# Where the output products stand among the seven products of a channel mixer's group

## The chip, the cores and the metric

The kernel runs on one core of a Trainium2 chip. The core has a matrix engine (TensorE, PE in the profile, with its weight loads as PEld), a vector engine (VectorE, DVE), a scalar engine (ScalarE, ACT), GpSimd (POOL) and SyncE (SP), which here only issues transfers. Each engine works through its own list of instructions in order; one waits for another through semaphores. The metric is the time of one execution on the device in microseconds (us), lower is better.

## The reference

A decoder trunk of two layers on a sequence of 256 positions and a width of 1024, in float32. Each layer has a token mixer beside a cross-attention into 256 memory tokens, then a dense channel mixer, and after each a layer norm:

```python
sub = jnp.concatenate([mix, mem_out], axis=-1) @ w_mix_out[i]
x = layer_norm(ALPHA * x + sub, ln_mix_g[i], ln_mix_b[i])
x = layer_norm(ALPHA * x + swiglu(x, w_ffn_in[i], w_ffn_out[i]), ln_ffn_g[i], ln_ffn_b[i])

def swiglu(x, w_in, w_out):
    g, u = jnp.split(x @ w_in, 2, axis=-1)
    return (jax.nn.silu(g) * u) @ w_out
```

The hidden width of the channel mixer is 2816, eleven chunks of 256. The change concerns `swiglu` alone, in both layers.

## The kernel before

**Splitting.** Every float32 operand of a matmul is split into a high and a low float32r part: ScalarE copies the source into the high part (`split`, L229) and VectorE subtracts it from the source for the low part (L230). A product of two split operands takes three matmuls (`PASSES`). Weights come as units of 1 MB (`raw_...`, 128 x 2048), and each unit is split in two halves of 128 x 1024 (`spl_...`). `Stream` hands them out: the order of all halves is fixed in advance by `weight_halves`, which reads the list of steps, ten split halves can stand at a time (`HALF_BUFS`), and the load of a unit is issued as soon as its raw buffer is free (`load_ahead`). So VectorE and ScalarE work ahead of TensorE by up to ten halves.

**The channel mixer** (`Ffn`, tiles end in f in the first layer and in g in the second). `ffn_steps` writes the list of steps, which `run` carries out. Chunks 0, 1 and 10 are plain ("r" steps, `chunk_in`: tiles pf, pg). Chunks 2 to 9 go in four groups of two ("s" steps, `product`): seven products M1 to M7 stand for the eight of a 2 x 2 block product. Each product is two halves, 12 matmuls of 128 x 512. Three PSUM tiles take them: M2 goes to Y, M5 and M3 to Z, and M1, M6, M7 and M4 all to X. X is added to in place, and is read between the products:

```python
if m == "M1":
    self.m1 = kept("m1", self.X)          # ScalarE copy, L592
elif m == "M2":
    nc.vector.tensor_add(self.m1, self.m1, self.Y)      # L600
elif m == "M6":
    u2 = kept("u2", self.X)               # ScalarE copy, L592
    nc.vector.tensor_add(u2, u2, self.Z)  # L604
elif m == "M7":
    nc.vector.tensor_add(self.m5, self.m5, self.X)      # L607
elif m == "M4":
    nc.scalar.activation(sg, self.X, AF.Silu)           # L610
```

So M7 cannot add to X before ScalarE has copied it into u2, and M4 not before VectorE has added it to m5. The weights of M5, M6 and M4 are sums of quarters of the weight matrix, made in place on VectorE over 128 x 2048 (L184); M7's second quarter is added to its raw tile by a GpSimd transfer (L187). Quarters 11 and 21 have one raw buffer each; the others and the output weights share a ring of four.

**Output products** ("out" steps, `chunk_out`). The hidden values of a chunk are transposed ("tp") and multiplied by the output weights, in two steps for each chunk (c.0 and c.1), each one half and 12 matmuls, into four PSUM tiles (fof, fog) that stay open over the whole mixer. They read nothing of the group that they stand in: only hidden values of chunks before it.

**Order.** TensorE's instructions run in the order of the list. Those of the other engines and the transfers are put in order when the kernel is built, by a scheduler that follows the list and its own estimates; no line of the kernel sets it.

Of the kernel before, what the change touches and what calls it, by code (L numbers as in the profile page):

```python
# [50 lines left out]
def ffn_steps(l):  # L51

    steps, due, prev = [], [], []
    for kind, c in PLAN:
        new = [("out", p, k, (0, 1)) for p in prev for k in range(2)]
        if kind == "S":

            ins = [("s", c, m) for m in PRODUCTS]
            steps += [ins[0], ("tp",), *due, ins[1], *new[:-1][:1], *ins[2:4], *new[:-1][1:], *ins[4:]]
            due = new[-1:]  # L60
        else:
            ins = [("r", c, i, (0, 1)) for i in range(4)]
            if l == 1 and c == 0:

                steps += [*(("r", 0, i, (0,)) for i in range(4)), *(("r", 1, i, (0,)) for i in range(2)), ("x",)]
            elif l == 1 and c == 1:
                steps += [*(("r", 1, i, (0,)) for i in range(2, 4)), *(("r", 0, i, (1,)) for i in range(4)),
                          *(("r", 1, i, (1,)) for i in range(2)), ("tp",), *(("r", 1, i, (1,)) for i in range(2, 4)), *new]
            elif c == NFF - 1:
                steps += [ins[0], ("tp",), *due, *ins[1:], *(("out", NFF - 3, k, (0,)) for k in range(2)), ("tp",)]  # L70
            elif c:
                steps += [ins[0], ("tp",), ins[1], *new[:1], ins[2], *new[1:], ins[3]]
            else:
                steps += ins
        prev = [c, c + 1] if kind == "S" else [c]
    return steps


def weight_halves():

    e = [(f"v{i}", x) for i in range(4) for x in range(2)]

    def both(names):
        return [(n, x) for n in names for x in range(2)]

    def ffn(l):
        h = []
        for st in ffn_steps(l):
            k = None
            if st[0] == "r":  # L90
                k = (f"r{l}_{st[1]}_{'AB'[st[2] // 2]}", st[2] % 2)
            elif st[0] == "s":
                h += [(f"s{l}_{st[1]}", st[2], x) for x in range(2)]
            elif st[0] == "out":
                k = (f"w{l}_{st[1]}", st[2])
            if k and k not in h:
                h.append(k)
        return h + [k for k in both([f"w{l}_{c}" for c in range(NFF - 3, NFF)]) if k not in h]

    e += both(("qm0", "u0", "u1", "u2", "km0", "vm0", "o0_0", "o0_1", "o0_2", "o0_3", "km1", "vm1"))  # L100
    e += ffn(0)
    e += both(("bv0", "bv1", "bv2", "bv3", "qm1", *(f"qk{i}" for i in range(6)), "o1_0", "o1_1", "o1_2", "o1_3"))
    return e + ffn(1)
# [113 lines left out]
def build(nc, tc, ins, out):  # L217
    ET = mybir.EngineType
    with (
# [302 lines left out]
        class Ffn:  # L522
# [107 lines left out]
            def run(self, mid=None):  # L630
                for st in ffn_steps(self.l):
                    self.tp_tiles()
                    if st[0] == "r":
                        self.chunk_in(*st[1:])
                        if st[1:3] == (NFF - 1, 0):
                            stream.held = {"gb", "vbig"}
                            self.gb = load_gb(self.l, "ffn")
                    elif st[0] == "s":
                        self.product(*st[1:])
                    elif st[0] == "x":  # L640
                        mid()
                    elif st[0] == "tp":
                        if self.pending:
                            self.transposes()
                    else:
                        self.chunk_out(*st[1:])
                return self.gb
# [346 lines left out]
```

## Time and profile before

| what | us |
|---|---|
| median of 3 runs (587.42 to 589.22) | 588.98 |
| the profiled execution | 589.02 |
| span of its instructions | 587.3 |
| TensorE busy | 559.6 |
| VectorE busy | 501.2 |
| ScalarE busy | 360.0 |
| mean granted clock of TensorE | 0.995 |

The span goes from the first to the last instruction; 1.7 us of the execution lie outside it. Times in a timeline are us from the start of the span. A row of a timeline merges like instructions that follow each other: its second number is the time from the first start to the last end, and what stands in brackets is the idle time of the engine before it and what ended that. The group of chunks 4 and 5 of the first layer reaches from 154.4 to 187.8 us, the four groups of the first layer from 129.6 to 255 us, and those of the second from 420.7 to 548 us.

### The profile page before, as it was taken

The numbers are of one execution on the slowest core, as the hardware profiler recorded it, in microseconds if no ns is written. First come the engines' busy times: TensorE is split into PE (matmuls) and PEld (weight loads), VectorE is DVE, ScalarE is ACT, GpSimd is POOL, SyncE is SP. The second block draws the span as 40 slices with busy tenths as digits, with TensorE's granted clock in tenths as the row PEclk, the third lists the DMA queues.
The fourth block names the chain that finished last, engine by engine and source line by source line (L and its number), as shares of the span: only waits on it lengthen the run. The fifth ranks groups of instructions, "written<-read, shape, count | busy, mean of one in ns | idle before, by whom it ended". The sixth has DMA issues, their size and how long they took to land.

```text
span 587.3 us, 8087 instructions
## 1 busy us (share of the span) xinstructions
PE 559.6 (95%) x3064; PEld 478.5 (81%) x3064; DVE 501.2 (85%) x639; ACT 360.0 (61%) x550; POOL 21.8 (4%) x32
## 2 busy tenths in 40 slices
PE   8999999999898989989999999999988989899994
PEld 7999879887786868778999998788876868687784
DVE  5797989998999989864987887499999989899726
ACT  6757958666766657642476979375567467477400
POOL 2020000000000000000100000000000000000001
PEclk9999999999999999999999999999998999999999
DMA  8996777447676694863476232335376684857102
GB/s 288 397 368 246 261 296 259 172 81 286 166 287 183 215 278 152 288 214 143 148 287 256 100 111 105 143 145 214 73 282 148 224 261 160 295 147 286 60 1 72
DMA packets 21335, 118.88 MB, mean 202 GB/s; under 512 B 2352, under 2 KB 5552, under 8 KB 8880
## 3 DMA queue, kind: packets, MB, share of 16 engines
q1 hardware_dynamic: 19856, 109.72, 51.0%
q0 software_dynamic: 1152, 8.39, 7.8%
q8 instruction: 24, 0.39, 0.3%
q10 hardware_dynamic: 288, 0.26, 0.1%
q14 instruction: 15, 0.12, 0.1%
HBM read 117.31 MB, written 1.05 MB: 202 GB/s over the span
## 4 chain that ended last, share of the span: by engine, by line
PE 79%; DVE 12%; ACT 3%; issue 3%; DMA 2%; SPq 0%; POOLq 0%; ACTq 0%; DVEq 0%
PE fof L253 10%; PE fog L253 7%; PE Xg L253 6%; PE pf L253 6%; PE Xf L253 6%; PE opc L253 4%; PE opa L253 4%; PE qk L253 3%; DVE spl_s_M L230 3%; PE Zf L253 3%; PE pg L253 3%; PE pu L253 3%; PE bv L253 3%; PE Zg L253 3%; PE pvm L253 3%
## 5 line engine op out<-in xcount | busy, mean ns | idle before, releaser
L230 DVE TENSOR_TENSOR spl_s_M<-raw_s,spl_s_M 128x1024 fp32r<-128x1024 f32 x112 | 131.8, 1219 | 8.6 <-ACT spl_s_M L229 8.6
L229 ACT CAST spl_s_M<-raw_s 128x1024 fp32r<-128x1024 f32 x112 | 112.1, 1048 | 40.9 <-DVE raw_s L184 16.2
L253 PE MATMUL fof<-spl_w,htf 128*128 128x512 f32 x264 | 63.2, 392 | 0.0
L253 PEld LDWEIGHTS fof<-spl_w,htf 128*128 128x128 f32 x264 | 49.1, 188 | 10.0
L230 DVE TENSOR_TENSOR spl_w<-raw_w,spl_w 128x1024 fp32r<-128x1024 f32 x44 | 53.3, 1218 | 4.4 <-ACT spl_w L229 4.3
L184 DVE TENSOR_TENSOR raw_s<-raw_s,raw_s 128x2048 f32<-128x2048 f32 x24 | 54.9, 2286 | 0.2
L253 PE MATMUL fog<-spl_w,htg 128*128 128x512 f32 x228 | 54.5, 392 | 0.0
L229 ACT CAST spl_w<-raw_w 128x1024 fp32r<-128x1024 f32 x44 | 46.0, 1053 | 9.5 <-PE Xf L253 3.4
L253 PEld LDWEIGHTS fog<-spl_w,htg 128*128 128x128 f32 x228 | 42.4, 188 | 8.7
L253 PE MATMUL qk<-x2T,spl_qk 128*128 128x256 f32 x288 | 36.7, 285 | 0.0
L253 PEld LDWEIGHTS qk<-x2T,spl_qk 128*128 128x128 f32 x288 | 35.2, 192 | 0.0
L253 PE MATMUL Xg<-spl_s_M,x3T 128*128 128x512 f32 x96 | 24.7, 415 | 5.1 <-DVE m5g L607 5.1
L253 PE MATMUL Xf<-spl_s_M,x1T 128*128 128x512 f32 x96 | 23.1, 395 | 5.6 <-DVE m5f L607 5.6
L253 PEld LDWEIGHTS Xg<-spl_s_M,x3T 128*128 128x128 f32 x96 | 18.9, 200 | 10.8 <-DVE m5g L607 6.8
L253 PE MATMUL Xg<-spl_s_M,SgM 128*128 128x512 f32 x96 | 23.6, 395 | 3.5 <-ACT u2g L592 3.5
L253 PEld LDWEIGHTS Xf<-spl_s_M,x1T 128*128 128x128 f32 x96 | 17.7, 188 | 10.8 <-DVE m5f L607 7.3
L253 PE MATMUL Xf<-spl_s_M,SfM 128*128 128x512 f32 x96 | 23.6, 395 | 2.7 <-ACT u2f L592 2.7
L253 PEld LDWEIGHTS Xg<-spl_s_M,SgM 128*128 128x128 f32 x96 | 17.7, 188 | 8.8 <-ACT u2g L592 5.2
L253 PEld LDWEIGHTS Xf<-spl_s_M,SfM 128*128 128x128 f32 x96 | 17.7, 188 | 7.9 <-ACT u2f L592 4.4
L253 PE MATMUL opc<-spl_o,mix 128*128 128x512 f32 x96 | 23.5, 397 | 0.0
L253 PE MATMUL Zg<-spl_s_M,SgM 128*128 128x512 f32 x96 | 23.2, 390 | 0.0
L253 PE MATMUL Zf<-spl_s_M,SfM 128*128 128x512 f32 x96 | 23.2, 390 | 0.0
(236 smaller groups left out, 1104.9 us busy)
## 6 DMA issues: line engine op xcount, KB each, us to landing
raw_s<-in_w SPq DMA_DIRECT2D x32, 1024.0 KB, 4.9
raw_w<-in_w SPq DMA_DIRECT2D x22, 1024.0 KB, 4.8
raw_o<-in_w SPq DMA_DIRECT2D x8, 1024.0 KB, 6.7
raw_s<-in_w POOLq DMA_DIRECT2D x8, 1024.0 KB, 8.3
raw_r_A<-in_w SPq DMA_DIRECT2D x6, 1024.0 KB, 4.8
raw_r_B<-in_w SPq DMA_DIRECT2D x6, 1024.0 KB, 4.7
raw_qk<-in_w SPq DMA_DIRECT2D x6, 1024.0 KB, 4.8
raw_u<-in_w SPq DMA_DIRECT2D x3, 1024.0 KB, 9.2
```

What stands on the lines that cost most here:

```text
L184: self.nc.vector.tensor_add(self.raw[parts[0]], self.raw[parts[0]], self.raw[parts[1]])
L229: nc.scalar.copy(hi, src)
L230: nc.vector.tensor_sub(lo, src, hi.bitcast(F32))
L253: nc.tensor.matmul(o, lhsT, rhs, start=start, stop=stop, skip_group_check=on)
```

## The change

Only `ffn_steps` differs. In each group the last three of the output products at hand are kept for the group's end: one stands between M6 and M7, one between M7 and M4, and one is left for the next group, behind its M1 and its transposes. The output products of chunk 0, which stood inside chunk 1 or (second layer) behind it, move into the first group. No instruction is added or taken away. The change adds five lines, so a line of the kernel before from L230 on is five higher in the changed one (L230 is L235, L600 is L605).

```diff
         if kind == "S":
             ins = [("s", c, m) for m in PRODUCTS]
-            steps += [ins[0], ("tp",), *due, ins[1], *new[:-1][:1], *ins[2:4], *new[:-1][1:], *ins[4:]]
-            due = new[-1:]
+            due += new
+            early, due = due[:-3], due[-3:]
+            steps += [ins[0], ("tp",), *early[:1], ins[1], *early[1:], *ins[2:5], due[0], ins[5], due[1], ins[6]]
+            due = due[2:]
         else:
             ...
             elif l == 1 and c == 1:
                 steps += [*(("r", 1, i, (0,)) for i in range(2, 4)), *(("r", 0, i, (1,)) for i in range(4)),
-                          *(("r", 1, i, (1,)) for i in range(2)), ("tp",), *(("r", 1, i, (1,)) for i in range(2, 4)), *new]
+                          *(("r", 1, i, (1,)) for i in range(2)), ("tp",), *(("r", 1, i, (1,)) for i in range(2, 4))]
+                due = new
             ...
             elif c:
-                steps += [ins[0], ("tp",), ins[1], *new[:1], ins[2], *new[1:], ins[3]]
+                steps += [ins[0], ("tp",), *ins[1:]]
+                due = new
```

The list for the first groups and the group of chunks 4 and 5, in both layers (outC.K is half K of the output product of chunk C):

```text
before  ... out0.0 ... out0.1 ... | M1 tp M5 out1.0 M2 M3 M6 M7 M4 | M1 tp out1.1 M5 out2.0 M2 M3 out2.1 out3.0 M6 M7 M4 | ...
after   ...                       | M1 tp out0.0 M5 M2 M3 M6 out0.1 M7 out1.0 M4 | M1 tp out1.1 M5 out2.0 M2 M3 M6 out2.1 M7 out3.0 M4 | ...
```

TensorE in the group of chunks 4 and 5 of the second layer, at the end of M6. In a name such as spl_s1_4_M6_1 stand the layer, the group, the product and the half; spl_w1_2_1 is the second half of chunk 2's output weights. Before:

```order
L253 MATMUL Xg4_4194<-spl_s1_4_M6_1_4365,SgM60_3887 128x512 x2
L253 MATMUL Xg4_4194<-spl_s1_4_M6_1_4365,SgM61_3888 128x512
L253 MATMUL Xg4_4194<-spl_s1_4_M7_0_4378,SgM70_3891 128x512 x2
L253 MATMUL Xg4_4194<-spl_s1_4_M7_0_4378,SgM71_3892 128x512
L253 MATMUL Xg4_4194<-spl_s1_4_M7_0_4378,SgM70_3891 128x512 x2
```

Now:

```order
L258 MATMUL Xg4_4196<-spl_s1_4_M6_1_4335,SgM60_3887 128x512 x2
L258 MATMUL Xg4_4196<-spl_s1_4_M6_1_4335,SgM61_3888 128x512
L258 MATMUL fog00_4011<-spl_w1_2_1_4348,htg2_4223 128x512
L258 MATMUL fog01_4012<-spl_w1_2_1_4348,htg2_4223 128x512
L258 MATMUL fog00_4011<-spl_w1_2_1_4348,htg2_4223 128x512
```

Behind M6 came M7, which adds to the same tile X; now out2.1 comes, 12 matmuls into other tiles.

VectorE in the same group, from the output halves or M3's last half to the first split of M7. Before:

```order
L230 TENSOR_TENSOR spl_w1_2_1_4325<-raw_w1_2_4179,spl_w1_2_1_4325 128x1024
L230 TENSOR_TENSOR spl_w1_3_0_4340<-raw_w1_3_4236,spl_w1_3_0_4340 128x1024
L184 TENSOR_TENSOR raw_s1_4_11_4175<-raw_s1_4_11_4175,raw_s1_4_22_4234 128x2048
L184 TENSOR_TENSOR raw_s1_4_21_4181<-raw_s1_4_21_4181,raw_s1_4_11_4175 128x2048
L230 TENSOR_TENSOR spl_s1_4_M6_0_4356<-raw_s1_4_11_4175,spl_s1_4_M6_0_4356 128x1024
L600 TENSOR_TENSOR m1g4_4215<-m1g4_4215,Yg4_4195 128x512
L230 TENSOR_TENSOR spl_s1_4_M6_1_4365<-raw_s1_4_11_4175,spl_s1_4_M6_1_4365 128x1024
L230 TENSOR_TENSOR spl_s1_4_M7_0_4378<-raw_s1_4_12_4177,spl_s1_4_M7_0_4378 128x1024
```

Now:

```order
L235 TENSOR_TENSOR spl_s1_4_M3_1_4316<-raw_s1_4_22_4183,spl_s1_4_M3_1_4316 128x1024
L189 TENSOR_TENSOR raw_s1_4_11_4175<-raw_s1_4_11_4175,raw_s1_4_22_4183 128x2048
L605 TENSOR_TENSOR m1g4_4217<-m1g4_4217,Yg4_4197 128x512
L189 TENSOR_TENSOR raw_s1_4_21_4181<-raw_s1_4_21_4181,raw_s1_4_11_4175 128x2048
L235 TENSOR_TENSOR spl_s1_4_M6_0_4326<-raw_s1_4_11_4175,spl_s1_4_M6_0_4326 128x1024
L235 TENSOR_TENSOR spl_s1_4_M6_1_4335<-raw_s1_4_11_4175,spl_s1_4_M6_1_4335 128x1024
L235 TENSOR_TENSOR spl_w1_2_1_4348<-raw_w1_2_4179,spl_w1_2_1_4348 128x1024
L235 TENSOR_TENSOR spl_s1_4_M7_0_4363<-raw_s1_4_12_4177,spl_s1_4_M7_0_4363 128x1024
```

The splits of M6 stand two halves earlier, and the addition of M2's result to m1 (which reads Y), with the sum for M4 (raw_s1_4_21) behind it, now stands ahead of M6's first split instead of behind it. The groups of chunks 6 and 8 of the second layer have the same order.

VectorE in the same group at the additions to u2 and m5. Before:

```order
L604 TENSOR_TENSOR u2g4_4374<-u2g4_4374,Zg4_4196 128x512
L184 TENSOR_TENSOR raw_s1_6_11_4410<-raw_s1_6_11_4410,raw_s1_6_12_4412 128x2048
L605 SCALAR_TENSOR_TENSOR m1g4_4215<-m1g4_4215,u2g4_4374 128x512
L607 TENSOR_TENSOR m5g4_4270<-m5g4_4270,Xg4_4194 128x512
L230 TENSOR_TENSOR spl_s1_6_M5_0_4487<-raw_s1_6_11_4410,spl_s1_6_M5_0_4487 128x1024
```

Now:

```order
L609 TENSOR_TENSOR u2g4_4344<-u2g4_4344,Zg4_4198 128x512
L235 TENSOR_TENSOR spl_w1_3_0_4382<-raw_w1_3_4236,spl_w1_3_0_4382 128x1024
L610 SCALAR_TENSOR_TENSOR m1g4_4217<-m1g4_4217,u2g4_4344 128x512
L235 TENSOR_TENSOR spl_s1_4_M4_0_4398<-raw_s1_4_21_4181,spl_s1_4_M4_0_4398 128x1024
L235 TENSOR_TENSOR spl_s1_4_M4_1_4407<-raw_s1_4_21_4181,spl_s1_4_M4_1_4407 128x1024
L612 TENSOR_TENSOR m5g4_4270<-m5g4_4270,Xg4_4196 128x512
```

Between the additions to u2 and to m5 stand three splits and one small product instead of one sum of 128 x 2048 and the small product.

## The prediction

> **What bounds the kernel now.** First the page's head, its busy times and the engines of the chain of waits:
>
> ```profile
> span 587.3 us, 8087 instructions
> PE 559.6 (95%) x3064; PEld 478.5 (81%) x3064; DVE 501.2 (85%) x639; ACT 360.0 (61%) x550; POOL 21.8 (4%) x32
> PE 79%; DVE 12%; ACT 3%; issue 3%; DMA 2%; SPq 0%; POOLq 0%; ACTq 0%; DVEq 0%
> ```
>
> TensorE carries 79% of the chain that ended last, and is idle for 587.3 - 559.6 = 27.7 us. Its own waits, longest first (us in total, times, longest):
>
> ```profile
> PE Xf L253 <- DVE m5f L607: 5.6, 4, 1.7
> PE Xg L253 <- DVE m5g L607: 5.1, 4, 2.1
> PE Xg L253 <- ACT u2g L592: 3.5, 4, 1.5
> PE Xf L253 <- ACT u2f L592: 2.7, 4, 0.7
> ```
>
> 16.9 of the 27.7 us are two waits in each of the eight groups: M7 for ScalarE's copy of X, and M4 for VectorE's addition of X to m5. What they cost in starts, the timeline of TensorE tells, here from M6 of the first layer's second group to M6 of its third, ahead of it the first group's M6, behind it the last group:
>
> ```profile
> 143.66 2.88 PE L253 MATMUL Xf<-spl_s_M,SfM 128*128 128x512 f32 x12
> ...
> 177.04 2.88 PE L253 MATMUL Xf<-spl_s_M,SfM 128*128 128x512 f32 x12
> 180.60 3.02 PE L253 MATMUL Xf<-spl_s_M,SfM 128*128 128x512 f32 x12 [0.68 <-ACT u2f L592]
> 184.91 5.74 PE L253 MATMUL Xf<-spl_s_M,x1T 128*128 128x512 f32 x24 [1.30 <-DVE m5f L607]
> 190.49 0.27 PE L620 MATMUL tpf<-ident,m1f 128*128 128x128 f32 x1
> ...
> 191.26 0.27 PE L620 MATMUL tpf<-ident,m5f 128*128 128x128 f32 x1
> ...
> 205.01 5.60 PE L253 MATMUL fof<-spl_w,htf 128*128 128x512 f32 x24
> 210.45 2.88 PE L253 MATMUL Xf<-spl_s_M,SfM 128*128 128x512 f32 x12
> ...
> 243.84 2.88 PE L253 MATMUL Xf<-spl_s_M,SfM 128*128 128x512 f32 x12
> ...
> 254.96 2.89 PE L253 MATMUL pf<-spl_r_A,x1T 128*128 128x512 f32 x12
> ```
>
> Two output products take 210.45 - 205.01 = 5.44, so a block of 12 matmuls 2.72 us. M7 starts 180.60 - 177.04 - 2.72 = 0.84 late, M4 184.91 - 180.60 - 2.72 = 1.59 late. A stretch from M6 to M6 holds eleven blocks, 29.92, and eight transposes at 0.11 (190.49 to 191.26), 0.88: 30.80 us of work. It takes 33.41. The second layer:
>
> ```profile
> 434.79 2.88 PE L253 MATMUL Xg<-spl_s_M,SgM 128*128 128x512 f32 x12
> 439.15 3.06 PE L253 MATMUL Xg<-spl_s_M,SgM 128*128 128x512 f32 x12 [1.48 <-ACT u2g L592]
> 444.31 7.33 PE L253 MATMUL Xg<-spl_s_M,x3T 128*128 128x512 f32 x24 [2.10 <-DVE m5g L607]
> ...
> 471.41 2.88 PE L253 MATMUL Xg<-spl_s_M,SgM 128*128 128x512 f32 x12
> ...
> 537.83 2.88 PE L253 MATMUL Xg<-spl_s_M,SgM 128*128 128x512 f32 x12
> 541.38 3.02 PE L253 MATMUL Xg<-spl_s_M,SgM 128*128 128x512 f32 x12 [0.68 <-ACT u2g L592]
> 545.18 3.01 PE L253 MATMUL Xg<-spl_s_M,x3T 128*128 128x512 f32 x12 [0.78 <-DVE m5g L607]
> 548.03 2.89 PE L253 MATMUL pg<-spl_r_A,x3T 128*128 128x512 f32 x12
> ```
>
> Here the first stretch takes 36.62, the two after it 33.21 each. At 444.31, 24 matmuls take 7.33 and not 5.74, and the windows by stretch show why, and VectorE beside it:
>
> ```profile
> core 0: us, PE busy (x) PEld busy (x) DVE busy (x) ACT busy (x) POOL busy (x), PEclk, DMA share, GB/s
> 440.00:450.00 10.00, 7.90 (x28) 6.02 (x27) 9.27 (x10) 5.88 (x7) 0.86 (x1) 0.83 0.81 204
> 191.53:224.95 33.42, 31.45 (x142) 25.45 (x141) 31.65 (x29) 21.24 (x26) 0.89 (x1) 1.00 0.68 220
> 485.72:518.93 33.21, 31.43 (x141) 25.44 (x141) 31.55 (x29) 21.00 (x26) 0.88 (x1) 1.00 0.69 222
> ```
>
> The granted clock falls to 0.83 there, behind two waits of 1.48 and 2.10. And VectorE is busy for 31.65 of 33.42 us of a group: it is nearly full, and needs 0.85 more than TensorE's 30.80. So the gain hangs on what VectorE lets through.
>
> **The waits that go.** An output product of 2.72 now stands ahead of M7 and another ahead of M4. Its hidden values are transposed blocks before, in the same group. What it must cover, the timeline of ScalarE and VectorE tells: the copy into u2 and the addition to m5 in the first layer's second group, the sums and splits behind them, and then, with TensorE's M3, the second layer's first and second groups:
>
> ```profile
> 179.96 0.58 ACT L592 COPY u2f<-Xf 128x512 f32<-128x512 f32 x1 [4.13 <-PE Xf L253]
> 184.18 0.68 DVE L607 TENSOR_TENSOR m5f<-m5f,Xf 128x512 f32<-128x512 f32 x1
> 194.52 4.61 DVE L184 TENSOR_TENSOR raw_s<-raw_s,raw_s 128x2048 f32<-128x2048 f32 x2
> 199.05 3.49 DVE L230 TENSOR_TENSOR spl_s_M<-raw_s,spl_s_M 128x1024 fp32r<-128x1024 f32 x3
> 428.31 4.63 DVE L230 TENSOR_TENSOR spl_s_M<-raw_s,spl_s_M 128x1024 fp32r<-128x1024 f32 x4
> 461.93 1.22 DVE L230 TENSOR_TENSOR spl_s_M<-raw_s,spl_s_M 128x1024 fp32r<-128x1024 f32 x1
> 463.25 2.88 PE L253 MATMUL Zg<-spl_s_M,SgM 128*128 128x512 f32 x12
> 463.45 0.69 DVE L600 TENSOR_TENSOR m1g<-m1g,Yg 128x512 f32<-128x512 f32 x1 [0.30 <-PE Yg L253]
> 464.06 5.76 DVE L230 TENSOR_TENSOR spl_s_M<-raw_s,spl_s_M 128x1024 fp32r<-128x1024 f32 x5
> ```
>
> M6's block is over at 177.04 + 2.72 = 179.76, ScalarE's copy of X at 180.54: 0.8 later, inside the 2.72 of the first output product. For m5, VectorE's new order puts three splits and one small product between u2 and m5. One split in a run takes 1.14 ((5.76 - 0.08) / 5, the last one's longer end, 1.22 instead of 1.14, taken off), a small operation 0.6 (463.45 to 464.06). From the end of M6 that is 0.8 for the copy, 0.6 for u2, 3 x 1.14 for the splits, 0.6 for the product, 5.4, and 0.7 for the addition itself: 6.1. TensorE reaches M4 after out, M7 and out, 8.16. So both waits are covered, the second by 2 us, as long as VectorE is not late at u2. Behind m5 on VectorE stand three splits, the next sum and the last product into m5, for which the next group's transposes wait: 6.1 + 3.4 + 2.3 + 0.7 = 12.5 behind M6, and TensorE gets there after out, M7, out, M4 and M1, 13.6. That holds too, by 1.1. If the covers fail, the old 0.84 and 1.59 come back in each group.
>
> What this is worth, in starts of TensorE. First layer: three stretches from 143.66 to 243.84 take 100.18 instead of 3 x 30.80 = 92.40, 7.8 too much; the last group's M6, M7 and M4 take 254.96 - 243.84 = 11.12 instead of 3 x 2.72 = 8.16, 3.0. Together 10.8. Second layer: the first stretch 36.62 - 30.80 = 5.8, which holds 1.6 of clock (7.33 - 5.74); two more, 2 x (33.21 - 30.80) = 4.8; the last group 548.03 - 537.83 - 8.16 = 2.0. Together 12.6. **Gone at most: 23.4 us.** That the output products of chunk 0 move past chunk 1 changes no block's length: TensorE had no wait there.
>
> The rule that bears on the clock is in the Trainium skill, page "TensorE: Matmul & The Clock Gate", section "Why this matters for your kernels": only idle gaps over about 3 us halve it. The trace disagrees, gaps of 1.48 and 2.10 did. By that rule I could not count on the 1.6, and the sum would be 21.8.
>
> **What stands in their place.** M6 moves two blocks (5.44) ahead on TensorE, its splits two halves (2 x 1.14 = 2.28) on VectorE: their lead shrinks by 3.2. In the first layer M6's first half was ready at 199.05 + 1.22 = 200.27 for a start at 210.45: 10.2 of lead. It pays 3.2 and three times 0.85, 5.8 in all. So in the first layer nothing is lost; the bounds are nothing and the 5.1 of the first rival below.
>
> In the second layer VectorE adds M2's result to m1 ahead of M6's first split, and the sum for M4 stands between. Nothing of this can start before M2 ends, however far VectorE is ahead. M3 starts at 463.25 on TensorE; m1 starts at 463.45, 0.20 later. Then come m1 with 0.61 (464.06 - 463.45), the sum with 2.27 (half of 199.05 - 194.52) and the split with 1.22: M6 can start 4.30 behind M3's start instead of 2.72. **A new wait of 1.58** in the groups of chunks 4, 6 and 8. With it a stretch is 32.4, more than the 31.55 that VectorE needs, so nothing is added for VectorE's load. Queued behind m1 on VectorE are M6's splits, for which TensorE waits, then M7's. In the second layer's first group both sums stand ahead of m1: 0.20 + 0.61 + 1.22 is under 2.72, but the lead is short there: the half was ready at 428.31 + 1.22 = 429.53 for 434.79, 5.3, less 3.2 leaves 2.1, and the earlier start takes from it too. Between 0 and 1.6 I take the middle, 0.8. In the first layer m1 stands behind M6's splits, or has the split alone behind it: 2.0, hidden. Given back: 3 x 1.58 + 0.8 = 5.5 (bounds: nothing, and 8 x 1.58 = 12.6 if every group gets it).
>
> **Transfers.** Their number stays; the loads of quarter 22 and of an output unit change places on SyncE's queue. They land 4.9 us after issue, GpSimd's sums 8.3:
>
> ```profile
> raw_s<-in_w SPq DMA_DIRECT2D x32, 1024.0 KB, 4.9
> raw_s<-in_w POOLq DMA_DIRECT2D x8, 1024.0 KB, 8.3
> ```
>
> Between M5's sum and M7's first split stand ten splits and a sum, over 13 us, which covers the 8.3. Between the sum that frees quarter 11 and the next M1 stand more splits than before. I take 0; uncovered, a group pays at most the difference, some 3 us.
>
> **Sum:** 23.4 - 5.5 = 17.9, against the profiled 589.02 (its span plus 1.7) 571.1; the median of the runs, 588.98, gives the same. I predict **571 us**.
>
> **Rivals.** *VectorE sets the pace in the first layer too.* For it: 31.65 busy of 33.42; against it: the lead of 10.2. If its three stretches stay at 31.65, the first layer gains 100.18 - 94.95 + 3.0 = 8.2 instead of 10.8, and the whole 15.3: 573.7. If half of VectorE's 1.77 us of waits stays as well, they are 32.5, the gain 5.7 (the 5.1 less of above) and the whole 12.8: 576.2. Trainium skill, "Perfetto Trace Analysis", "Identifying the Most-Contended Engine": occupancy tells for VectorE how near it is to its limit, and the most contended engine is the one to relieve. By that page this is the case to expect; the waits of TensorE in the trace speak against it.
>
> *All waits go and none comes.* VectorE would have to be done with m1, the sum and the split within M3's 2.72. Against it stand the three durations; for it only that M2's last matmuls may count as ended sooner than I read: 589.0 - 23.4 = 565.6.
>
> *Slower: M6 starves in every group.* M6's splits have lost two halves of lead, and VectorE takes its work in order: if it comes late to m1 as a whole, M6 waits for all that is queued ahead of its first split. Two splits more than the chain of 4.30 make a wait of 4.30 + 2.28 - 2.72 = 3.9; in all eight groups 31, less the 23.4 gone: 596.6. It decides from 23.4 / 8 = 2.9 a group; there the change comes to nothing. For it: the lead of 2.1 in the second layer's first group, with a VectorE that is full; against it the leads of the first layer, and that the wait itself lets VectorE catch up.
>
> *The change does not take the waits for m5 away*, because VectorE comes to u2 over 2 us late, behind the splits that M6 waited for: 1.59 is then left in each group, 12.7 of the 17.9: 583.8.
>
> **Numbers.** Forecast 0.65 (its own range 568.5 to 574), VectorE's pace 0.18, all gone 0.08, m5 late 0.04, slower 0.03, nothing 0.02. Half of "all gone", the last three and a tail of the second lie outside 566 to 578, under 2 in 10; its ends are the bounds 589.0 - 23.4 and 589.0 - 23.4 + 12.6. Under 0.3% (1.8 us) cannot be told from no change here; so faster 0.95, same 0.02, slower 0.03.
>
> **What would show it.** The rows of waits for u2 and m5 gone; stretches from M6 to M6 of about 30.9 in the first layer and 32.4 in the second; a new wait of M6 for spl_s_M of about 1.6 three times in the second layer; granted clock 1.00 around M4. Wrong if first-layer stretches exceed 31.7, if TensorE waits for m5 again, or if M6 waits there too.

## The result and the profile after

The changed kernel takes 571.48 us (median of 4 runs, 571.07 to 572.14) where the kernel before took 588.2 in the same comparison: a ratio of 0.9718, 95% interval 0.9693 to 0.9743. The profiled execution took 571.07, its span is 17.9 us shorter than before's.

The head of the page, the engines of the chain of waits, and TensorE's longest wait (us in total, times, longest), after the change:

```profile
span 569.4 us, 8025 instructions
PE 554.5 (97%) x3064; PEld 478.1 (84%) x3064; DVE 499.4 (88%) x639; ACT 358.5 (63%) x550; POOL 22.1 (4%) x32
PE 86%; DVE 9%; ACT 2%; issue 1%; DMA 1%; SPq 0%; POOLq 0%; ACTq 0%
PE Xg L258 <- DVE spl_s_M L235: 3.9, 4, 1.2
```

The four rows of waits for u2 and m5, 16.9 us, are gone from both layers. One row is new: in the second layer, once in each group, the product into X waits for a split of its weights. What else TensorE waits for, by these rows, belongs to the token mixers and the start of the kernel, at most 1.1 us in one row. Where the new wait shows, the timeline of TensorE tells: M6 of the four groups of the first layer and what follows the last one's M4, then M6 with the output product behind it and one M4 of the second layer, and the end of its last group:

```profile
137.96 2.88 PE L258 MATMUL Xf<-spl_s_M,SfM 128*128 128x512 f32 x12
...
168.78 2.88 PE L258 MATMUL Xf<-spl_s_M,SfM 128*128 128x512 f32 x12
...
199.62 2.88 PE L258 MATMUL Xf<-spl_s_M,SfM 128*128 128x512 f32 x12
...
230.44 2.92 PE L258 MATMUL Xf<-spl_s_M,SfM 128*128 128x512 f32 x12
...
244.07 2.89 PE L258 MATMUL pf<-spl_r_A,x1T 128*128 128x512 f32 x12
...
418.47 0.39 PE L258 MATMUL Xg<-spl_s_M,SgM 128*128 128x512 f32 x1
419.27 2.83 PE L258 MATMUL Xg<-spl_s_M,SgM 128*128 128x512 f32 x11 [0.42 <-DVE spl_s_M L235]
421.94 2.88 PE L258 MATMUL fog<-spl_w,htg 128*128 128x512 f32 x12
...
430.10 5.61 PE L258 MATMUL Xg<-spl_s_M,x3T 128*128 128x512 f32 x24
...
450.03 0.39 PE L258 MATMUL Xg<-spl_s_M,SgM 128*128 128x512 f32 x1
451.60 2.79 PE L258 MATMUL Xg<-spl_s_M,SgM 128*128 128x512 f32 x11 [1.18 <-DVE spl_s_M L235]
454.22 2.88 PE L258 MATMUL fog<-spl_w,htg 128*128 128x512 f32 x12
...
482.35 0.39 PE L258 MATMUL Xg<-spl_s_M,SgM 128*128 128x512 f32 x1
...
514.63 0.39 PE L258 MATMUL Xg<-spl_s_M,SgM 128*128 128x512 f32 x1
...
529.70 2.89 PE L258 MATMUL pg<-spl_r_A,x3T 128*128 128x512 f32 x12
```

In the first layer the stretches from M6 to M6 take 30.82, 30.84 and 30.82 us, TensorE's own work. In the second they take 31.56, 32.32 and 32.28: M6 runs its first matmul, which needs only the high part of the split (ScalarE's copy), and then stands still until VectorE has made the low part. M6's block, up to the output product behind it, takes 454.22 - 450.03 = 4.19 instead of 2.72, so the wait costs 1.47; in the first group 0.75. The windows of one stretch of each layer:

```profile
core 0: us, PE busy (x) PEld busy (x) DVE busy (x) ACT busy (x) POOL busy (x), PEclk, DMA share, GB/s
199.62:230.44 30.82, 30.82 (x142) 25.60 (x140) 29.63 (x28) 18.74 (x24) 0.89 (x1) 1.00 0.71 236
450.03:482.35 32.32, 31.14 (x142) 25.53 (x140) 31.52 (x29) 21.16 (x26) 0.84 (x1) 1.00 0.68 226
```

In this stretch of the first layer TensorE has no gap left (busy for 30.82 of 30.82 us). In the second VectorE is busy for 31.5 of 32.3 us, and the granted clock is 1.00.

### The profile page after: what moved, and what is told of

It reads as the page before. It is cut to its first block, busy times and chain, and to the rows that moved or that the text cites. A ratio compares the mean times of both kernels' runs of the same rounds, so it can differ in the third digit from the quotient of the medians.

```text
span 569.4 us, 8025 instructions
## 1 busy us (share of the span) xinstructions
PE 554.5 (97%) x3064; PEld 478.1 (84%) x3064; DVE 499.4 (88%) x639; ACT 358.5 (63%) x550; POOL 22.1 (4%) x32
## 4 chain that ended last, share of the span: by engine, by line
PE 86%; DVE 9%; ACT 2%; issue 1%; DMA 1%; SPq 0%; POOLq 0%; ACTq 0%
PE fof L258 11%; PE fog L258 9%; PE Xf L258 8%; PE Xg L258 7%; PE pf L258 6%; PE opc L258 4%; PE opa L258 4%; PE Zf L258 4%; PE qk L258 4%; PE pg L258 3%; PE pu L258 3%; PE bv L258 3%; PE pvm L258 3%; PE va L258 3%; DVE raw_s L189 2%; DVE spl_s_M L235 2%
## 5 line engine op out<-in xcount | busy, mean ns | idle before, releaser
L234 ACT CAST spl_s_M<-raw_s 128x1024 fp32r<-128x1024 f32 x112 | 114.2, 1052 | 44.7 <-DVE raw_s L189 35.3
L235 DVE TENSOR_TENSOR spl_s_M<-raw_s,spl_s_M 128x1024 fp32r<-128x1024 f32 x112 | 132.1, 1219 | 4.9 <-ACT spl_s_M L234 4.6
L235 DVE TENSOR_TENSOR spl_w<-raw_w,spl_w 128x1024 fp32r<-128x1024 f32 x44 | 52.9, 1218 | 0.0
L258 PE MATMUL Xg<-spl_s_M,x3T 128*128 128x512 f32 x96 | 22.6, 389 | 0.0
L258 PE MATMUL opa<-spl_o,mix 128*128 128x512 f32 x96 | 22.5, 392 | 0.0
```

The lines of the kernel that those rows point to most:

```text
L234: nc.scalar.copy(hi, src)
L235: nc.vector.tensor_sub(lo, src, hi.bitcast(F32))
L258: nc.tensor.matmul(o, lhsT, rhs, start=start, stop=stop, skip_group_check=on)
```

## The experiments

Where an experiment is said to start from the changed kernel, its diff is against that; from the kernel before, against before. "Stretch" is from M6 to M6, "chain" and "pace" are the two explanations of the new wait that the expectations name.

### One layer alone

The new rules of the list of steps hold for one layer, the other keeps the old ones (shown from the changed kernel; the piece for chunk 0's products, not shown, is old in the other layer too):

```diff
-            due += new
-            early, due = due[:-3], due[-3:]
-            steps += [ins[0], ("tp",), *early[:1], ins[1], *early[1:], *ins[2:5], due[0], ins[5], due[1], ins[6]]
-            due = due[2:]
+            if l == 0:      # l == 1 in the second kernel
+                ...the four lines
+            else:
+                ...the two lines of before
```

> The new order of the output products in the first layer alone; the second layer keeps the order of before. The prediction: the first layer gains 10.8 (two waits in each of four groups) with nothing given back, so 588.5 - 10.8 = 577.7, stretches from M6 to M6 30.8 in the first layer, and 36.6, 33.2, 33.2 as before in the second. Rival (the layers share the gain: VectorE arrives at the second layer without lead and its waits grow): over 579.

> The new order in the second layer alone. The prediction: 12.6 gone less 5.5 given back, 588.5 - 7.1 = 581.4, stretches 31.6, 32.3, 32.3 in the second layer with a wait for M6's splits of 1.47 in each of its last three groups. Rival (the second layer's new wait comes from the first layer's faster pace): no wait at M6 here, 576.5.

The first layer alone: 578.31 us (577.54 to 578.36), ratio to before 0.9819 (0.9804 to 0.9833). The second alone: 581.68 (581.17 to 582.16), ratio 0.9879 (0.9864 to 0.9894). Before took 588.82 beside them, so the gains are 10.5 and 7.1, 17.6 together, where the whole change gave 16.7 between the medians of its own comparison and 17.9 between the profiled executions: within that spread the layers add up. The second layer's new wait is the same with the first layer's old pace; TensorE's wait in the kernel with the second layer alone:

```profile
PE Xg L261 <- DVE spl_s_M L238: 3.9, 4, 1.2
```

### One place alone

One output product of each group moves, to one of the two places; chunk 0's stay (from the kernel before):

```diff
-            steps += [ins[0], ("tp",), *due, ins[1], *new[:-1][:1], *ins[2:4], *new[:-1][1:], *ins[4:]]
+            steps += [ins[0], ("tp",), *due, ins[1], *new[:-2], *ins[2:5], new[-2], *ins[5:]]   # M6 out M7
+            steps += [ins[0], ("tp",), *due, ins[1], *new[:-2], *ins[2:6], new[-2], *ins[6:]]   # M7 out M4
```

> The kernel before with one output product of each group moved between M6 and M7, none between M7 and M4; chunk 0's output products stay. M7's lateness goes (0.84 in seven groups, 1.64 in one: 7.5), M4's stays (1.6 in the first layer's groups, 1.4 in the second's). Theory 'each wait is the path from its own product': 581.0, or 579.4 where the granted clock stays at 1.00 in the second layer's first group, with only one gap ahead of M4. Rival 'VectorE's pace': M4 then waits for m5 longer by part of what M7 gained, since VectorE comes to u2 and m5 behind the splits: up to 584.

> The kernel before with one output product of each group moved between M7 and M4, none between M6 and M7; chunk 0's output products stay. M4's lateness goes (1.6, 1.6, 1.6, 2.0 in the first layer, 2.4, 1.4, 1.4, 1.1 in the second, and 1.6 of clock: 14.7), M7's 0.84 stays in each group. Theory 'each wait is the path from its own product': 588.5 - 14.7 = 573.8. Rival 'VectorE's pace': the stretch with the one wait left, 30.8 + 0.84 = 31.64, is what VectorE needs anyway (31.5), so no wait at M6 for its splits here, and the second product moved (the whole change) brings 2.3 in addition, not 7.5. Against both: if M4's wait only moves to M7 or M6, 580 and over.

Between M6 and M7 alone: 578.48 (577.96 to 579.36), ratio 0.9826. Between M7 and M4 alone: 574.57 (574.34 to 574.71), ratio 0.9758. TensorE's waits, of the first and then of the second:

```profile
PE Xg L253 <- DVE m5g L607: 5.7, 4, 1.7
PE Xf L253 <- DVE m5f L607: 4.1, 4, 1.7
```

```profile
PE Xg L253 <- ACT u2g L592: 3.4, 4, 1.2
PE Xf L253 <- ACT u2f L592: 2.7, 4, 0.7
```

Each place takes away its own wait and leaves the other, as the first theory had it. But the two do not add up. Alone, the place ahead of M4 gains 14.2 us and the other 10.3, some 25 together, and both in one kernel some 17: the second place adds 3.1, not the 7.5 of the first theory, and the rival, VectorE's pace, had expected 2.3. The first kernel is 0.9 under the 579.4 that was expected for a granted clock of 1.00 in the second layer's first group (M4's 24 matmuls take 5.74 there). M4's wait shrank in the first layer (0.8 instead of 1.3 in three groups) and grew in the last three groups of the second (1.70, 1.70 and 1.50 instead of 1.11, 1.10 and 0.78), as the rival had it. Now the second kernel's M6, and what it tells of the whole change:

```profile
173.07 2.88 PE L253 MATMUL Xf<-spl_s_M,SfM 128*128 128x512 f32 x12
...
204.89 2.88 PE L253 MATMUL Xf<-spl_s_M,SfM 128*128 128x512 f32 x12
...
248.53 2.89 PE L253 MATMUL pf<-spl_r_A,x1T 128*128 128x512 f32 x12
...
457.96 2.88 PE L253 MATMUL Xg<-spl_s_M,SgM 128*128 128x512 f32 x12
...
489.78 2.88 PE L253 MATMUL Xg<-spl_s_M,SgM 128*128 128x512 f32 x12
```

A stretch is 31.8 in both layers (only the second layer's first takes 32.31). The whole change makes 30.8 of it in the first layer but 32.3 in the second's later groups. There the product between M6 and M7 takes away what M7's wait costs, 31.82 - 30.82 = 1.0, and brings the wait of 1.47: a loss of 0.5 in each of the later stretches. What the second place adds to the first, 574.57 to 571.48, comes from the first layer, whose groups end 248.53 - 244.07 = 4.5 us earlier; the second layer's take 0.6 longer. The order "both places in the first layer, only the one ahead of M4 in the second" was not run.

### Chunk 0's products stay

Both places are filled, but the output products of chunk 0 stand where they stood before (the other two pieces of the change are undone):

```diff
-            due += new
-            early, due = due[:-3], due[-3:]
+            early, late = (due + new)[:-3], (due + new)[-3:]
-            ... *ins[2:5], due[0], ins[5], due[1], ins[6]]
+            ... *ins[2:5], late[0], ins[5], late[1], ins[6]]
-            due = due[2:]
+            due = late[2:]
```

> Both places of each group are filled as in the changed kernel, but the output products of chunk 0 stay where they were before; so the first group has out1.0 and out1.1 alone, and the second has none left over to stand ahead of its own, right behind its transposes. The prediction put the move of chunk 0's products at nothing by itself: 571.5 within 0.6. Rival ('the move supplies the output product that covers the split of the hidden values behind the second group's transposes'): TensorE waits there for hidden values, 1 to 2 us in each layer, and the time is 572.5 to 575.5, unless VectorE uses these waits to catch up.

571.09 us (570.64 to 571.88), ratio 0.9714 (0.9691 to 0.9736): no difference from the whole change. TensorE waits in a place that the whole change does not have, for hidden values behind the second group's transposes (here in the second layer), and at M6 of the last group (the second layer again):

```profile
440.92 1.20 PE L254 MATMUL fog<-spl_w,htg 128*128 128x512 f32 x4 [0.31 <-ACT htg L230]
...
516.28 2.79 PE L254 MATMUL Xg<-spl_s_M,SgM 128*128 128x512 f32 x11 [1.17 <-DVE spl_s_M L231]
```

So the rival's mechanism is there, 0.3 in the first layer and 0.7 in the second, but costs nothing in the whole: the wait of 1.17 at M6, three times there in the changed kernel, now comes in full only in the last group. What TensorE loses ahead, it does not lose later.

### What makes the new wait: the chain, or VectorE's pace

The prediction put M6's wait down to a chain: M2 ends, m1 is added, the sum for M4 is made, M6 is split, 4.3 us where M3 gives 2.72. The rival: VectorE simply needs a stretch of 32.3, its 31.5 of work and a wait of 0.57 for ScalarE. Four kernels tell them apart, all from the changed kernel. The first takes the chain away and leaves the work (cut to the addition; ScalarE's silu of m1 moves with it):

```diff
-                    nc.vector.tensor_add(self.m1, self.m1, self.Y)          # under M2
+                    with tc.issue_after(stream.low[f"s{self.l}_{c}", "M6", 1].ins):
+                        nc.vector.tensor_add(self.m1, self.m1, self.Y)      # under M6, behind its split
```

> The changed kernel (571.5 us) with one edge more in VectorE's order: the addition of M2's result to m1 is issued behind M6's second split, in both layers, so that neither it nor M2's end stands ahead of M6's splits. VectorE's work stays the same. Theory 'chain' (the prediction's): the second layer's M6 waits (0.75 in its first group, 1.47 in each of the three others, 5.2 us in starts) only because M2's end, m1, the sum for M4 and the split follow each other; they go, its stretches from M6 to M6 fall from 32.3 to 30.9, and the time to 566.3. Theory 'pace': VectorE's own work (31.5 us busy in a stretch, and about 0.7 of waiting that its order holds) sets the stretch; it stays between 31.6 and 32.3, TensorE waits as long or in another place, and the time is 569.5 to 571.5.

571.14 us (570.61 to 571.85). Its windows, VectorE's one wait in such a stretch, and M6 there:

```profile
450.13:482.23 32.10, 31.39 (x142) 25.48 (x140) 31.50 (x29) 20.99 (x26) 0.84 (x1) 1.00 0.71 228
...
468.27 1.23 DVE L235 TENSOR_TENSOR spl_s_M<-raw_s,spl_s_M 128x1024 fp32r<-128x1024 f32 x1 [0.57 <-ACT spl_s_M L234]
...
451.20 2.81 PE L258 MATMUL Xg<-spl_s_M,SgM 128*128 128x512 f32 x11 [0.68 <-DVE spl_s_M L235]
```

The stretch falls by 0.2 only, to 32.10, which is VectorE's 31.50 of work and its wait of 0.57: VectorE's pace. M6 waits less, but M6 was only the place where TensorE met VectorE. The second kernel leaves the chain and takes work away (the product into m1, 0.6 us, goes to GpSimd; edges, which force an order on the scheduler and are not shown here, hold VectorE's order as it was in the second layer's last three groups):

```diff
-                    nc.vector.tensor_add(u2, u2, self.Z)
-                    nc.vector.scalar_tensor_tensor(self.m1, self.m1, -1.0, u2, ALU.mult, ALU.mult)
+                    nc.vector.scalar_tensor_tensor(u2, u2, -1.0, self.Z, ALU.mult, ALU.subtract)
+                    nc.gpsimd.tensor_mul(self.m1, self.m1, u2)
```

> The changed kernel with the product into m1 (0.6 us on VectorE in each group) moved to GpSimd, its sign put into the addition to u2; in the second layer's groups of chunks 4, 6 and 8 edges hold VectorE's order m1, sum for M4, first split of M6 as it was. So VectorE has 0.6 us less to do in a group, and the chain behind M2's end is unchanged. Chain: the wait of 1.47 stays in the three groups, stretches 32.3, time 571.5 (within 0.5). Pace: the wait shrinks by the 0.6 to some 0.9, stretches 31.7, time 569.7.

571.14 us (570.89 to 571.66), with the chain in the timeline of VectorE and TensorE:

```profile
447.53 2.88 PE L268 MATMUL Zg<-spl_s_M,SgM 128*128 128x512 f32 x12
447.73 0.69 DVE L615 TENSOR_TENSOR m1g<-m1g,Yg 128x512 f32<-128x512 f32 x1 [0.39 <-PE Yg L268]
448.34 2.29 DVE L197 TENSOR_TENSOR raw_s<-raw_s,raw_s 128x2048 f32<-128x2048 f32 x1
450.54 2.35 DVE L244 TENSOR_TENSOR spl_s_M<-raw_s,spl_s_M 128x1024 fp32r<-128x1024 f32 x2
451.81 2.79 PE L268 MATMUL Xg<-spl_s_M,SgM 128*128 128x512 f32 x11 [1.17 <-DVE spl_s_M L244]
...
450.25:482.56 32.31, 31.14 (x141) 25.53 (x140) 31.31 (x28) 20.95 (x26) 5.28 (x2) 1.00 0.68 228
```

VectorE is ahead now and waits 0.39 for M2's result, and M6 still waits 1.17: the chain is real, and alone it gives 32.3. So both theories were half right: two limits lie 0.2 us apart, and taking away either one uncovers the other. The third kernel is the same product on GpSimd without the edges, in which the scheduler puts both sums ahead of m1 and so shortens the chain to 2.0 us as well:

> The same product on GpSimd, without edges: in the second layer's groups of chunks 4, 6 and 8 VectorE's order now has both sums ahead of m1 and only the split of M6 behind it, so the chain behind M2's end is 2.0 us, under M3's 2.72, and VectorE has 0.6 us less to do in a group. Chain: the three waits of 1.47 go, stretches 30.9, time 567.1 (the first group's 0.75 stays). Pace: 0.6 less in each, about 0.9 left, stretches 31.7, time 569.7.

569.96 us (569.52 to 571.03), stretches of 31.91:

```profile
450.31:482.22 31.91, 31.14 (x141) 25.53 (x140) 31.30 (x28) 20.90 (x26) 5.28 (x2) 1.00 0.69 230
```

31.30 of work and 0.58 of waiting for ScalarE: pace. But VectorE's busy time fell by 0.2 and not by 0.6; GpSimd's help is dear, as the fourth kernel shows.

### The sum for M4 on GpSimd

```diff
-            self.nc.vector.tensor_add(self.raw[parts[0]], self.raw[parts[0]], self.raw[parts[1]])
+            (self.nc.gpsimd if key[1] == "M4" else self.nc.vector).tensor_add(
+                self.raw[parts[0]], self.raw[parts[0]], self.raw[parts[1]])
```

> The changed kernel with the sum for M4 (128 x 2048, 2.27 us on VectorE) made by GpSimd instead, in all eight groups. It takes the sum out of the chain behind M2's end (2.0 us left, under M3's 2.72) and 2.27 us from VectorE's 31.5 in a group, so both theories expect the waits of M6 to go: stretches 30.9 in both layers, 566.3. The sum has some 8 us until M4's first split in the second layer (448 to 458 us in the changed kernel). If GpSimd takes longer than that, or if VectorE's own operations grow longer beside it, M4 waits instead: with 10 us and more a group would lose some 2 us, and the time be 571 or over.

586.12 us (583.0 to 587.79), 14.6 over the changed kernel and some 20 over what both theories expected. The sum itself is done in time. But look at the group of all these sums on GpSimd, at one of them and the splits of M6 that meet it, and at M4 of the first layer's second group:

```profile
L189 POOL TENSOR_TENSOR raw_s<-raw_s,raw_s 128x2048 f32<-128x2048 f32 x8 | 39.5, 4936 | 87.2 <-DVE raw_s L189 67.6 <-ACT htf L235 11.3 <-PE pf L259 8.3
...
455.64 4.58 POOL L189 TENSOR_TENSOR raw_s<-raw_s,raw_s 128x2048 f32<-128x2048 f32 x1 [11.38 <-DVE raw_s L189]
456.57 5.87 DVE L236 TENSOR_TENSOR spl_s_M<-raw_s,spl_s_M 128x1024 fp32r<-128x1024 f32 x2 [0.17 <-ACT spl_s_M L235]
461.36 4.13 PE L259 MATMUL Xg<-spl_s_M,SgM 128*128 128x512 f32 x11 [2.74 <-DVE spl_s_M L236]
...
183.15 7.37 PE L259 MATMUL Xf<-spl_s_M,x1T 128*128 128x512 f32 x24 [2.12 <-DVE m5f L613]
```

A pair of splits takes 2.35 us alone and 5.87 here: it starts 0.9 after GpSimd's sum, and its first split is there for M6 at 461.36, one split's 1.14 after the sum's end (455.64 + 4.58 = 460.22). 2.27 us were taken from VectorE, and 3.5 given back, right ahead of M6, which waits 2.0 to 2.8 in the second layer's four groups. That is not the whole loss: of the 16.1 us between the profiled executions 6.3 are lost by the end of the first layer's groups (250.40 instead of 244.07), where M4 waits for m5, as the expectation had allowed for, and 10.1 in the second layer's, of which 0.4 come back behind them. The granted clock takes part in both: 24 matmuls take 7.37 behind the wait of 2.12, and M6's last eleven 4.13 behind that of 2.74. The Trainium skill, "SBUF — State Buffer", section "SBUF: two separate sides", says that VectorE's operations with two inputs in SBUF and GpSimd's share a port pair that one of them holds for its whole instruction while the other blocks; this trace agrees, the split that met the sum ended 1.14 after it.

### Less waiting for VectorE

VectorE's wait of 0.57 comes from the sum for M5: ScalarE cannot begin M5's split before the whole sum is done, and on VectorE only the small product into m5 (0.6) stands between the sum and that split's low part. Made in two operations, the first half can go ahead:

```diff
-            self.nc.vector.tensor_add(self.raw[parts[0]], self.raw[parts[0]], self.raw[parts[1]])
+            for cols in (slice(0, n), slice(n, 2 * n)) if key[1] in ('M5',) else (slice(0, 2 * n),):
+                self.nc.vector.tensor_add(self.raw[parts[0]][:, cols], self.raw[parts[0]][:, cols], self.raw[parts[1]][:, cols])
```

> The changed kernel with the sum for M5 (128 x 2048) made in two operations of 128 x 1024, so that ScalarE can begin with M5's first half while VectorE sums the second: the wait of VectorE for ScalarE (0.57 in each stretch of the second layer) goes, VectorE's busy time grows by one operation's start (under 0.1). In the resulting order m1 stands behind both sums, so M2's end is no longer the limit. Pace: stretches of 31.6 to 31.8 in the second layer instead of 32.3, 569.5. If only the chain had held it: 30.9, 567.1. If the wait for ScalarE moves to the next split: 571.

569.78 us (569.41 to 570.12), ratio to before 0.9692 (0.9671 to 0.9714). Two combinations: with the product on GpSimd, and, all on VectorE, with m1 behind M6's split and M2 ahead of the output product behind M5:

```diff
-            steps += [ins[0], ("tp",), *early[:1], ins[1], *early[1:], *ins[2:5], ...
+            steps += [ins[0], ("tp",), *early[:1], *ins[1:3], *early[1:], *ins[3:5], ...
```

> The sum for M5 in two, and the product into m1 on GpSimd. Pace: VectorE's 31.5 less 0.6 is 30.9, TensorE's own 30.8: waits at M6 under 0.3 in the second layer, 567.0 to 568.0. If GpSimd's product holds VectorE up by 0.5 in each group (one split pair took 2.86 instead of 2.35 beside it): 569.

> Nothing moved to GpSimd: M2 stands ahead of the output product behind M5, m1 is issued behind M6's second split, and M5's sum is made in two. The chain behind M2's end is gone, VectorE's wait for ScalarE too, its work is unchanged. Pace: stretches 31.5 in the second layer, 571.1 - 3 x 0.57 = 569.4, and no kernel without less work for VectorE goes below. If VectorE's work were not the limit: 566.5.

569.44 us (569.23 to 569.7), near the 569 expected if GpSimd's product holds VectorE up, and 569.36 (569.01 to 569.87), the 569.4 expected of VectorE's pace. One stretch of each of the three, in this order:

```profile
481.53:513.32 31.79, 31.11 (x141) 25.52 (x140) 31.62 (x30) 21.02 (x27) 0.88 (x1) 1.00 0.70 231
```

```profile
482.78:514.10 31.32, 31.13 (x142) 25.53 (x140) 31.29 (x29) 21.06 (x26) 5.37 (x2) 1.00 0.71 236
```

```profile
481.10:512.70 31.60, 31.14 (x141) 25.52 (x140) 31.45 (x30) 21.09 (x26) 0.88 (x1) 1.00 0.75 233
```

In all three the stretch is VectorE's busy time and 0.2 us or less: 31.62 of 31.79, 31.29 of 31.32, 31.45 of 31.60. That is the pace itself, with the chain and the wait for ScalarE out of the way. The second gains 1 us in the stretches, but not in the whole: it pays 0.8 us in the first layer, where the transposes wait for m5, and reaches the second layer's first M6 1.9 us later than the first of the three. The third beats the kernel before (ratio 0.9684, 0.9662 to 0.9705). It also beats the changed kernel by 2.1 us in the medians: the fastest run of that, 571.07, is over its slowest, and so is the fastest, 570.64, of the kernel with chunk 0's products left, which ran beside it. The two ratios to before overlap in their intervals (0.9693 to 0.9743 for the changed kernel), so the gain rests on these times alone.

## Why the prediction was right, and where it was not

**The total.** 571 was predicted, 571.48 measured; against the profiled execution 571.1 and 571.07. By terms, in starts of TensorE: up to the end of the first layer's last group 254.96 - 244.07 = 10.9 were gained, where 10.8 stood; in the second layer 548.03 - 529.70 - 10.9 = 7.4, where 12.6 - 5.5 = 7.1 stood. 0.4 is lost behind 529.70, of which the prediction had nothing (39.3 us from there to the end before, 39.7 after).

**The waits that go.** Both products cover what they should: the rows for u2 and m5 are gone, and each place alone takes away its own wait. TensorE waits for u2 or m5 nowhere in the changed kernel.

**The clock.** M4 of the second layer's first group takes 5.61 for its 24 matmuls, not 7.33, and the 1.6 us counted for it came back. In the kernel that changes the first layer alone two such gaps, 1.44 and 2.14, stand in the second layer, and M4's 24 matmuls take 7.34.

**The new wait.** Its place, its count and nearly its size were right: 1.47 three times and 0.75 once, 5.2, where 1.58 and 0.8, 5.5, stood. The 0.1 is M6's first matmul (0.23), which does not need the low part and goes ahead, less 0.13 that the others then take longer. The kernel with the chain kept shows the mechanism by itself. What was too generous is the sentence that the stretch of 32.4 is "more than the 31.55 that VectorE needs". VectorE needs 31.5 and 0.57 of waiting for ScalarE that its order holds, 32.1. The chain, 32.3, decided by 0.2 us, not by 0.85; a reader who had removed it on the strength of that sentence would have expected 5 us and got 0.3.

**The lead in the first layer: the step that failed.** "It pays 3.2 and three times 0.85, 5.8 in all" was to leave M6's splits over 4 us ahead. After the change: M6's two splits on VectorE in the first group (M6 at 137.96) and in the last (M6 at 230.44), the window from the first of them to the first of those, and VectorE's two longest waits in it:

```profile
125.82 2.36 DVE L235 TENSOR_TENSOR spl_s_M<-raw_s,spl_s_M 128x1024 fp32r<-128x1024 f32 x2
...
229.27 2.35 DVE L235 TENSOR_TENSOR spl_s_M<-raw_s,spl_s_M 128x1024 fp32r<-128x1024 f32 x2
...
127.04:230.49 103.45, 103.45 (x471) 85.84 (x469) 98.25 (x89) 67.54 (x81) 2.62 (x3) 1.00 0.67 222
...
DVE spl_s_M L235 <- ACT spl_s_M L234: 2.0, 3, 1.2
DVE u2f L609 <- ACT u2f L597: 1.9, 1, 1.9
```

The first split is ready 10.9 us ahead of M6 in the first group (125.82 + 1.22 against 137.96) and 0.05 too late in the last. 11.0 are used up, just what was there: 103.45 us pass on VectorE between the two splits, 92.48 on TensorE from M6 to M6. VectorE is busy for 98.25 of them, 5.8 more than TensorE takes. That this is the prediction's 5.8 is in part chance: some 2.3 of it is VectorE's longer stretch, three times 0.76 (0.85 stood there), and 3.5 come from one more sum for M4 (2.27), one more addition to m1 and one more split of hidden values (0.6 each) than three groups hold, since these stand behind M6's first split in the first group and ahead of it in the last. The prediction's 3.2 was the move of M6 itself. The other 5.2 are VectorE's own idle time, which it did not count. It took the lead for a store that only VectorE's work draws on, but VectorE works in order and stands still: at u2 and at the product into m5 for ScalarE's reading of X (1.9 and 0.9), which comes after M6 and M4 on TensorE, and behind its sums for ScalarE's splits (2.0), however far ahead its own splits are. The first layer lost nothing because it has four groups and not five. The step was wrong, and that its result held, to 0.05 us, was luck.

**The rivals.** "VectorE sets the pace in the first layer too" had the right engine. In the first layer it did not come true, and with the lead used up it would have from a fifth group on, which no run here has; in the second layer VectorE's need lies 0.2 us under what decides. Judged by the section of the Trainium skill that the prediction weighed against TensorE's waits ("Perfetto Trace Analysis", "Identifying the Most-Contended Engine"), VectorE is the engine to relieve; the traces after the change agree, it is busy for 31.5 of 32.3 us there, and the further 1.7 and 2.1 us found here came with taking its wait for ScalarE away. "M6 starves in every group" did not happen: M6 waits in the second layer alone, and the wait stays at 1.47 from group to group. "All waits go and none comes" and "m5 late" did not happen.

**The transfers** show no part in it: no wait of TensorE or VectorE in these stretches is put down to one. Only ScalarE waits for them, 4.2 us in three waits in the second layer's groups.

## What to carry to other kernels

An engine's need in a stretch is its busy time and the waits that its own order holds, not the busy time alone: compare that sum with the other engines' before saying which limit comes next. When two limits lie within some tenths of a microsecond, removing either one shows next to nothing, and only an experiment that removes both, or one that relieves one and holds the other, tells what is there. A lead of an engine that works in order is not a store: each operation that waits for the engine it runs ahead of ties it back, so the lead at the last group has to be read, not carried over from the first.

## What was not expected of the hardware

GpSimd beside VectorE: a sum of 128 x 2048 took GpSimd 4.94 us (VectorE: 2.28), and two splits beside it 5.87 instead of 2.35; a product of only 128 x 512 took GpSimd 4.4 us in the second layer, where VectorE is nearly full. In these runs an operation moved from one to the other did not come off the first's time in full: of 0.6 us moved, 0.2 were won; of 2.27 moved, more than all came back.

The granted clock. In the kernel with the sum on GpSimd, M6 stands still for 2.02 to 2.76 us in the second layer. Windows behind the waits of 2.74, 2.76 and 2.30:

```profile
461.00:465.00 4.00, 3.64 (x10) 2.92 (x11) 4.00 (x5) 1.74 (x2) 0.00 (x0) 0.59 0.33 92
530.00:535.00 5.00, 5.00 (x12) 3.93 (x13) 5.00 (x5) 1.28 (x3) 0.00 (x0) 0.50 0.49 133
427.00:431.00 4.00, 3.51 (x15) 2.91 (x16) 4.00 (x5) 1.55 (x3) 0.00 (x0) 1.00 0.29 78
```

One gap of 2.74 or 2.76 was followed by a clock of 0.59 and 0.50, one of 2.30 was not. But in the first layer of the same kernel one gap of 2.12 was followed by 24 matmuls in 7.37 instead of 5.61, and in the kernel before the change two gaps of 1.48 and 2.10, with a product of 3.06 between them, by 24 in 7.33. So a gap's length alone does not decide it in these traces; what does, no run here settles.
